# First product unit on the first quarter of x, idle products ahead of it, compression evacuation a slot later, sequences ahead of the recurrence

## The chip, the cores and the metric

The kernel runs on one core of a Trainium2 chip. The metric is the device time of one execution in microseconds. The kernel before was timed in three runs: median 2907.64 us, from 2907.31 to 2909.32. One more execution was taken by the hardware profiler; all timeline positions below are microseconds from the start of its span.

The engines are TensorE (PE in the rows; its weight loads are PEld), VectorE (DVE), ScalarE (ACT), GpSimd (POOL), and SyncE (SP), which only issues transfers. POOL issues some transfers too, on a queue of its own.

## The reference

One inference step through two layers of a hybrid decoder, all in fp32, for a prompt of 256 tokens and for 8 sample sequences of 8 new tokens each with 1024 cached tokens: 320 tokens (the N of the code), model width 2048.

```
x += layer0(norm(x)):   z = norm(x) @ w_in_e                 one projection, split into
        rx, rg              RG-LRU: conv4(rx), gates, a linear recurrence, times gelu(rg)
        q, kc,vc, ks,vs, kw,vw   attention: compressed blocks, selected blocks, window
        compress(k): per block of 64 tokens  gelu((k + pe) @ w1) @ w2      for k and for v
        out = concat(rnn, attention) @ w_out_e
x += ffn(norm(x));  x += shortconv(norm(x));  x += ffn(norm(x))       ffn: relu(x W1)^2 W2
```

For the 8 sample sequences the cached rows are in pages of 128 tokens, found through a page table. For each sequence the selected blocks, the window and the new tokens give scores, a softmax, and the weighted sum of the values.

## The kernel before, in words

**Products.** A large matrix product is `gemm` (L189). fp32 operands are held as a rounded high part and a low rest (`xh`, `xl` or `yh`, `yl` for the activations, `whi`, `wlo` for the weights), and each 128x128 block of weights takes three products of 320 columns (L204 to L206). A weight tile `wraw` of 512 KB is loaded by SP (`w_dma`, L129), then `w_conv` (L137) makes a half of it: ScalarE casts `whi` (L145), VectorE subtracts to get `wlo` (L146); for the first halves of the first four tiles GpSimd subtracts. A unit of the first layer's product is 4 chunks of the inner dimension by two blocks of 128 outputs, 24 products of TensorE. Every unit has a row of work for the other engines behind it.

**Slots and steps.** After a unit `gemm` calls `side()`, which counts up a slot and runs what `at(n, f, ...)` has registered for it, in the order of registration (L165 to L178). After every block of outputs it calls `step()`, which runs what `after(k, f)` has registered. Each engine keeps the order in which its instructions are issued; nothing reorders them later. So the order of registration is the order in which two pieces of work of one slot stand in an engine's queue.

**The start.** x comes in four quarters of 512 columns by three tensors (`xn`), with a weight tile between them. `feed(qt)` (L358) takes a quarter: `feed_a` (L341) transposes a chunk on TensorE (three transposes against the identity, the rows of L346), `feed_b` (L352) splits it into `yh` and `yl`. Quarters 0 and 1 are fed ahead of the first product, 2 and 3 behind the first and the second unit. `x_squares` sums x's squares for the norm.

**The compression.** `cmp_load_w` (L676) loads w1 and w2 for k or for v, `cmp_load` loads cached pages into `cx`, `cmp_swap` (L694) reorders them to `cy` by copies on VectorE, GpSimd and ScalarE, `cmp_mm` (L706) does 64 small products (L713) and evacuates them by ScalarE copies (L719) and VectorE adds (L720), twice each. The evacuations of q, k and v (`qr`, `kv`, L882 and L817) stand on VectorE in the same slots.

**Recurrence and sequences.** C0 = 42 is the first slot of the recurrence, which has four pairs of channel heads, eight slots apart: convolution at slots 4 and 5 behind the pair's first, gates at 5 and 6 (L584), decay at 6 (L590 to L596), scan in three parts (`rec_scan_a`, `_b`, `_c`) at 6, 7 and 8, gelu at 8 and 9, `rec_y` at 10. P4 = 65 is the first slot of the 8 sequences, three slots apart: `sa_kt` transposes cached keys to `ktl` (L1168), `sa_scores` (L1264) multiplies, `sa_softmax` (L1267) reduces and exponentiates, `sa_trans` (L1299) transposes the weights, `sa_pv` (L1312) multiplies by the values, `sa_ot` (L1335) turns the result. Where both have work in a slot (64 to 76), the recurrence, registered first, stands ahead. Slots 75 and 76 have no product unit; behind them the outputs are split and the next product, `gemm(8, 8)`, begins.

PSUM has three banks for the large products, four for the small ones (tag a) and one for others (tag o).

Of the kernel before, what the change touches and what calls it, by code (L numbers as in the profile page):

```python
# [15 lines left out]
ALU = mybir.AluOpType  # L16
# [4 lines left out]
NB = 8  # L21
# [49 lines left out]
def tile_hybrid_step(ctx: ExitStack, tc: tile.TileContext, A, O, stop=None, dbg=None):  # L71
# [57 lines left out]
    def w_dma():  # L129
        w, k, ku, c, width = units[st["dma"]]  # L130
        st["dma"] += 1
        r = wp.tile([128, UW], F32, name="wraw", bufs=NRAW)
        SP.dma_start(r[:, :ku * width].rearrange("p (k f) -> p k f", k=ku),
                     w[k * 128:(k + ku) * 128, c:c + width].rearrange("(k p) f -> p k f", p=128))
        raws.append(r)
# [29 lines left out]
    def at(n, f, *a):  # L165
        later.setdefault(n, deque()).append((f, a))
# [114 lines left out]
    for qt in range(4):  # L281
        for i in range(3):
            SP.dma_start(xn[i][:tn[i], qt * 512:(qt + 1) * 512], xsrc[i][:, qt * 512:(qt + 1) * 512])
        w_dma()
    V.memset(epst, EPS)
    S.activation(ssq[:, 0, 0:1], epst, AF.Sqrt)
    V.memset(ones, 1.0)
# [17 lines left out]


# [51 lines left out]
    def feed(qt):  # L358
        c = 4 * qt
        feed_a(c)  # L360
        feed_a(c + 1)
        if qt == 0:
            w_conv()
        feed_b(c)
        feed_a(c + 2)
        feed_b(c + 1)
        feed_a(c + 3)
        if qt == 0:
            w_conv()
        feed_b(c + 2)  # L370
        feed_b(c + 3)
# [85 lines left out]
    feed(1)  # L457
    for qt in range(3):
        at(qt, w_conv)
        at(qt, w_conv)  # L460
        if qt:
            at(qt, feed, qt + 1)
        at(qt, x_squares, qt)
    at(2, x_squares, 3)
    side(0)
# [210 lines left out]
    def cmp_load_w(i):  # L676
        nm_ = "kv"[i]
        for hf in range(2):
            SP.dma_start(w1[64 * hf:64 * hf + 64, i], A["cmp_w1_" + nm_][0][:, 32 * hf:32 * hf + 32])
        SP.dma_start(w2[64 * i:64 * i + 64, 64 * i:64 * i + 64], A["cmp_w2_" + nm_][0])  # L680
# [25 lines left out]
    def cmp_mm(bp, i, pages):  # L706
# [4 lines left out]
        for d in range(16):  # L711
            for u in range(2):
                PE.matmul(p[64 * u:64 * u + 64, :n], w1[:, i, 16 * u + d], y[:, 16 * u + d],  # L713
                          start=d == 0, stop=d == 15)
        nh = min(pages, 8)
        for k in range(pages // nh):
            h = hid[64 * i:64 * i + 64, 16 * bp + 8 * k:16 * bp + 8 * k + nh].rearrange("p n g s -> p s (n g)")
            q = p[:, 64 * k:64 * k + 8 * nh].rearrange("p (s n) -> p s n", s=2)
            S.copy(h, q[64 - 64 * i:128 - 64 * i])  # L719
            V.tensor_tensor(h, q[64 * i:64 * i + 64], h, ALU.add)  # L720
# [546 lines left out]
    def sa_softmax(b):  # L1267
# [26 lines left out]
        V.tensor_tensor(l[:, 0:2], l[:, 0:2], l[:, 2:4], ALU.add)  # L1294
        V.reciprocal(l[:, 0:2], l[:, 0:2])
        V.tensor_tensor(l[:, 0:2], l[:, 0:2], gs[:, 1:3, b], ALU.mult)
        sj["p", b] = (s, l)

    def sa_trans(b):  # L1299
# [3 lines left out]
        for i in range(4):  # L1303
            p = bank("a")
            n = min(4, 13 - 4 * i)
            for k in range(n):
                PE.transpose(p[:, 128 * k:128 * k + 128], s[:, 4 * i + k], ident)  # L1307
            (S.copy if i % 2 else V.tensor_copy)(
                t[:, 4 * i:4 * i + n].rearrange("p c k -> p (c k)"), p[:, :128 * n])
        G.tensor_scalar(t[:, 13], pcT, cm[:, C_BM + b:C_BM + b + 1], 1.0, op0=ALU.mult, op1=ALU.mult)  # L1310
# [64 lines left out]

    for pr in range(4):
# [8 lines left out]
        at(n + 8, rg_gelu_a, pr)  # L1385
        at(n + 9, rg_gelu_b, pr)
        at(n + 10, rec_y, pr)

    P4 = P3 + 20
    at(P4 - 1, sa_begin)  # L1390
    at(P4 + 1, sa_select)
    for b in range(NB + 1):
        n = P4 + 3 * b
        if b < NB:
            at(n, sa_kt, b, 0)
            at(n, sa_kt, b, 1)
        if b:
            at(n + 1, sa_trans, b - 1)
        if b < NB:
            at(n + 1, sa_kt, b, 2)  # L1400
            at(n + 2, sa_scores, b)
            at(n + 2, sa_softmax, b)
        if b:
            at(n + 2, sa_pv, b - 1)
            at(n + 4, sa_ot, b - 1)
# [286 lines left out]
```

## Time and profile before

| | |
|---|---|
| median of three runs | 2907.64 us |
| the profiled execution's own time | 2911.25 us |
| its span | 2909.6 us |
| TensorE busy | 2846.3 us, 98% of the span |
| VectorE, ScalarE, GpSimd busy | 1618.6 (56%), 1213.1 (42%), 378.2 (13%) |
| mean granted TensorE clock | 0.99 of full speed |
| mean DMA rate | 159 GB/s, 463.98 MB in all |

TensorE is busy for nearly all of the span, in the second half without a gap. In the first 600 us it is not: the products of the first layer stand there beside the attention's small work on the other engines. The granted clock is a share of full speed; of its two levels, 1.2 and 2.4 GHz, the profile's mean over a stretch is a mixture. The listed waits give the engine's instruction, the engine and instruction whose end it waited for, the sum in us, how often, and the longest.

### The profile page before, as it was taken

Reading aid. Unit: us, or ns where it says so; the run is one execution under the profiler, and the core shown is the slowest. Engines: PE = TensorE matmul, PEld = TensorE weight load, DVE = VectorE, ACT = ScalarE, POOL = GpSimd, SP = SyncE. Lnnn points to the kernel's source line nnn. Section 1 sums busy time; section 2 is a strip of 40 time slices with the busy share of each in tenths; the row PEclk is TensorE's granted clock in tenths of the full one; section 3 lists DMA queues with packets and bytes.
Section 4 is the critical chain, followed back from the end, with each engine's and each line's share of the span. In section 5 each row is a group of like instructions: output and inputs, shape, how many; then the busy total and the mean of one; then the engine's idle time right before and its main releaser. Section 6 shows DMA issues by size and latency. Waiting matters only on the chain.

```text
span 2909.6 us, 53661 instructions
## 1 busy us (share of the span) xinstructions
PE 2846.3 (98%) x20947; PEld 2785.6 (96%) x20947; DVE 1618.6 (56%) x2937; ACT 1213.1 (42%) x2336; POOL 378.2 (13%) x555
## 2 busy tenths in 40 slices
PE   8999987999999999999999999999999999999999
PEld 7998776899999999999999999999999999999999
DVE  6796677774444544544465555555444444544544
ACT  4555644354334434434443333344433433433433
POOL 2323353230010010010010111111011011001000
PEclk9999989999999999999999999999999999999999
DMA  8765258645445555555445444444444444544543
GB/s 244 213 198 156 73 147 257 210 138 162 165 154 167 165 159 161 165 166 153 153 144 156 152 147 150 147 153 148 149 152 145 153 152 149 149 152 148 149 157 119
DMA packets 275997, 463.98 MB, mean 159 GB/s; under 512 B 19050, under 2 KB 100694, under 8 KB 275215
## 3 DMA queue, kind: packets, MB, share of 16 engines
q1 hardware_dynamic: 268254, 438.47, 49.1%
q0 software_dynamic: 6864, 19.44, 2.1%
q8 instruction: 164, 2.69, 0.4%
q10 hardware_dynamic: 624, 2.64, 0.2%
q14 instruction: 91, 0.74, 0.1%
HBM read 452.95 MB, written 15.92 MB: 161 GB/s over the span
## 4 chain that ended last, share of the span: by engine, by line
PE 81%; DVE 0%; DMA 0%; ACT 0%; issue 0%; DVEq 0%; ACTq 0%
PE ps_g L204 27%; PE ps_g L206 27%; PE ps_g L205 27%; DMA wraw<-in_w_out_e_dram 0%; PE ps_a L1652 0%; DVE wlo L146 0%; PE ps_a L1264 0%; PE ps_o L1325 0%; PE ps_a L1307 0%; DVE ktl L1168 0%; PE ps_a L633 0%; PE ps_a L1624 0%; DVE rs L1473 0%; PE ps_a L436 0%; DVE y L1475 0%
## 5 line engine op out<-in xcount | busy, mean ns | idle before, releaser
L146 DVE TENSOR_TENSOR wlo<-wraw,whi 128x512 fp32r<-128x512 f32 x1488 | 1007.4, 718 | 1122.3 <-ACT whi L145 1121.5
L145 ACT CAST whi<-wraw 128x512 fp32r<-128x512 f32 x1492 | 854.1, 617 | 1377.8 <-PE ps_g L206 1334.0
L204 PE MATMUL ps_g<-yl,whi 128*128 128x320 f32 x3408 | 1066.9, 313 | 10.9 <-DVE kv L817 5.1
L205 PE MATMUL ps_g<-yh,wlo 128*128 128x320 f32 x3408 | 1056.8, 310 | 0.0
L206 PE MATMUL ps_g<-yh,whi 128*128 128x320 f32 x3408 | 1056.6, 310 | 0.0
L204 PE MATMUL ps_g<-xl,whi 128*128 128x320 f32 x2560 | 796.2, 311 | 11.3 <-DVE xl L446 7.3
L206 PE MATMUL ps_g<-xh,whi 128*128 128x320 f32 x2560 | 792.7, 310 | 0.0
L205 PE MATMUL ps_g<-xh,wlo 128*128 128x320 f32 x2560 | 792.7, 310 | 0.0
L204 PEld LDWEIGHTS ps_g<-yl,whi 128*128 128x128 f32 x3408 | 643.2, 189 | 22.3 <-issue 8.4
L205 PEld LDWEIGHTS ps_g<-yh,wlo 128*128 128x128 f32 x3408 | 643.3, 189 | 1.7 <-issue 0.2
L206 PEld LDWEIGHTS ps_g<-yh,whi 128*128 128x128 f32 x3408 | 643.2, 189 | 0.0
L204 PEld LDWEIGHTS ps_g<-xl,whi 128*128 128x128 f32 x2560 | 482.4, 188 | 13.1 <-DVE xl L446 7.7
L205 PEld LDWEIGHTS ps_g<-xh,wlo 128*128 128x128 f32 x2560 | 482.4, 188 | 0.0
L206 PEld LDWEIGHTS ps_g<-xh,whi 128*128 128x128 f32 x2560 | 482.1, 188 | 0.0
L1477 POOL TENSOR_TENSOR y<-y,rs 128x320 f32<-128x320 f32 x96 | 92.3, 994 | 1257.8 <-DVE rs L1473 1257.8
L1473 DVE TENSOR_TENSOR rs<-ps_g,r 128x320 f32<-128x320 f32 x128 | 60.6, 488 | 25.1 <-PE ps_g L206 25.0
L1506 DVE TENSOR_TENSOR fr<-fr 128x320 f32<-128x320 f32 x128 | 62.3, 487 | 11.1 <-ACT xh L1509 11.1
L431 POOL TENSOR_TENSOR nacc<-nacc,nsq 128x320 f32<-128x320 f32 x45 | 44.1, 980 | 172.0 <-ACT nsq L427 170.4
L1507 DVE TENSOR_TENSOR xl<-fr,xh 128x320 fp32r<-128x320 f32 x128 | 62.9, 492 | 4.4
L1509 ACT ACTIVATE xh<-fr 128x320 fp32r<-128x320 f32 x128 | 60.3, 471 | 4.1
L1503 ACT ACTIVATE fr<-ps_g 128x320 f32<-128x320 f32 x128 | 56.1, 438 | 5.7 <-PE ps_g L206 5.7
L1586 POOL TENSOR_TENSOR xx<-cg,r 128x256 f32<-128x256 f32 x16 | 13.1, 819 | 278.4 <-DVE xx L1584 278.4
(382 smaller groups left out, 1426.3 us busy)
## 6 DMA issues: line engine op xcount, KB each, us to landing
wraw<-in_w_ff_dram SPq DMA_DIRECT2D x512, 512.0 KB, 3.7
wraw<-in_w_in_o_dram SPq DMA_DIRECT2D x96, 512.0 KB, 3.7
wraw<-in_w_in_e_dram SPq DMA_DIRECT2D x74, 512.0 KB, 5.3
wraw<-in_w_out_e_dram SPq DMA_DIRECT2D x32, 512.0 KB, 5.5
wraw<-in_w_out_o_dram SPq DMA_DIRECT2D x32, 512.0 KB, 3.9
cx<-in_cache_cmp_k_dram SPq DMA_DIRECT2D x64, 128.0 KB, 2.1
cx<-in_cache_cmp_v_dram SPq DMA_DIRECT2D x64, 128.0 KB, 3.4
kl<-in_cache_sel_k_dram SPq DMA_DIRECT2D x64, 128.0 KB, 3.6
```

The lines of the kernel that those rows point to most:

```text
L145: S.copy(h, r)
L146: (G if u < 4 and hf == 0 else V).tensor_tensor(l, r, h.bitcast(F32), ALU.subtract)
L204: PE.matmul(ps[m][:, :N], wh, al, start=k + j == 0, stop=False)
L205: PE.matmul(ps[m][:, :N], wl, ah, start=False, stop=False)
L206: PE.matmul(ps[m][:, :N], wh, ah, start=False, stop=k + j == nk - 1)
L431: G.tensor_tensor(nacc["t"], nacc["t"], sq, ALU.add)
L1473: V.tensor_tensor(t, ps[:, :N], scale, ALU.mult)
L1477: after(1, lambda: G.tensor_tensor(y[:, c], y[:, c], t, ALU.add))
L1503: S.activation(t, ps[:, :N], AF.Relu)
L1506: V.tensor_tensor(t, t, t, ALU.mult)
L1507: V.tensor_tensor(xl[:, c], t, xh[:, c].bitcast(F32), ALU.subtract)
L1509: after(1, lambda: S.activation(xh[:, c], t, AF.Square))
```

## The change

Five parts.

First, the start: `ones` is filled first; `spin` issues products of 128x128 of `ones` by `ones` whose result nobody reads, ten at the head and one behind each chunk of quarter 0; quarters 1, 2 and 3 are fed from `after` steps 1, 3 and 5, so inside the first units; the first weight tile's transfer is two halves. Second, `cmp_load_w` uses GpSimd's queue. Third, `cmp_mm`'s evacuation is a function of its own, one copy and one add over both halves, in the next slot (the last one, of sequences 6 and 7 for v, directly). Fourth, the registration of the sequences stands ahead of that of the recurrence, and `sa_ot` a slot later in relation to `sa_trans`. Fifth, three small VectorE operations on `l` (the sum of the exps and its reciprocal, with the gates) move from the end of `sa_softmax` to the end of `sa_trans`.

```diff
@@ w_dma @@
+        nd = 2 if st["dma"] == 1 else 1
+        d = r[:, :ku * width].rearrange("p (k f) -> p k f", k=ku)
+        s_ = w[k * 128:(k + ku) * 128, c:c + width].rearrange("(k p) f -> p k f", p=128)
+        for i in range(0, ku, ku // nd):
+            SP.dma_start(d[:, i:i + ku // nd], s_[:, i:i + ku // nd])
...
@@ loads at the head @@
+    V.memset(ones, 1.0)
     V.memset(epst, EPS)
     S.activation(ssq[:, 0, 0:1], epst, AF.Sqrt)
-    V.memset(ones, 1.0)
...
+    idle = bank("o")
+
+    def spin(n):
+        for _ in range(n):
+            PE.matmul(idle[:, :128], ones, ones, start=True, stop=True)
+
+    spin(10)
+
     p0 = bank("a")
...
     def feed(qt):
         c = 4 * qt
-        feed_a(c)
-        feed_a(c + 1)
+        for i in range(4):
+            feed_a(c + i)
+            if qt == 0:
+                spin(1)
+            if i == 0 or i == 1 and qt:
+                w_conv()
+            if i:
+                feed_b(c + i - 1)
+        feed_b(c + 3)
         if qt == 0:
             w_conv()
-        feed_b(c)
-        feed_a(c + 2)
-        feed_b(c + 1)
-        feed_a(c + 3)
-        if qt == 0:
-            w_conv()
-        feed_b(c + 2)
-        feed_b(c + 3)
...
     feed(0)
-    feed(1)
+
+    for qt in range(1, 4):
+        after(2 * qt - 1, lambda qt=qt: feed(qt))
     for qt in range(3):
-        at(qt, w_conv)
-        at(qt, w_conv)
-        if qt:
-            at(qt, feed, qt + 1)
-        at(qt, x_squares, qt)
-    at(2, x_squares, 3)
-    side(0)
+        at(qt + 1, x_squares, qt)
+    at(3, x_squares, 3)
...
@@ cmp_load_w @@
-            SP.dma_start(w1[64 * hf:64 * hf + 64, i], A["cmp_w1_" + nm_][0][:, 32 * hf:32 * hf + 32])
-        SP.dma_start(w2[64 * i:64 * i + 64, 64 * i:64 * i + 64], A["cmp_w2_" + nm_][0])
+            G.dma_start(w1[64 * hf:64 * hf + 64, i], A["cmp_w1_" + nm_][0][:, 32 * hf:32 * hf + 32])
+        G.dma_start(w2[64 * i:64 * i + 64, 64 * i:64 * i + 64], A["cmp_w2_" + nm_][0])
...
@@ cmp_mm @@
+        if (bp, i) == (3, 1):
+            cmp_evac(bp, i, pages, p)
+        else:
+            at(st["slot"] + 1, cmp_evac, bp, i, pages, p)
+
+    def cmp_evac(bp, i, pages, p):
         nh = min(pages, 8)
-        for k in range(pages // nh):
-            h = hid[64 * i:64 * i + 64, 16 * bp + 8 * k:16 * bp + 8 * k + nh].rearrange("p n g s -> p s (n g)")
-            q = p[:, 64 * k:64 * k + 8 * nh].rearrange("p (s n) -> p s n", s=2)
-            S.copy(h, q[64 - 64 * i:128 - 64 * i])
-            V.tensor_tensor(h, q[64 * i:64 * i + 64], h, ALU.add)
+        h = hid[64 * i:64 * i + 64, 16 * bp:16 * bp + pages].rearrange("p (k n) g s -> p k s (n g)", n=nh)
+        q = p[:, :8 * pages].rearrange("p (k s n) -> p k s n", k=pages // nh, s=2)
+        S.copy(h, q[64 - 64 * i:128 - 64 * i])
+        V.tensor_tensor(h, q[64 * i:64 * i + 64], h, ALU.add)
...
@@ sa_softmax, sa_trans @@
-        V.tensor_tensor(l[:, 0:2], l[:, 0:2], l[:, 2:4], ALU.add)
-        V.reciprocal(l[:, 0:2], l[:, 0:2])
-        V.tensor_tensor(l[:, 0:2], l[:, 0:2], gs[:, 1:3, b], ALU.mult)
...
                 t[:, 4 * i:4 * i + n].rearrange("p c k -> p (c k)"), p[:, :128 * n])
+        V.tensor_tensor(l[:, 0:2], l[:, 0:2], l[:, 2:4], ALU.add)
+        V.reciprocal(l[:, 0:2], l[:, 0:2])
+        V.tensor_tensor(l[:, 0:2], l[:, 0:2], gs[:, 1:3, b], ALU.mult)
...
@@ the registrations of the slots (the loop over the sequences now ahead of the loop over pr) @@
+    rec_tail(3)
+    for b in range(NB + 1):
+        n = P4 + 3 * b
...
+        if b:
+            at(n + 1, sa_trans, b - 1)
+        if b > 1:
+            at(n + 1, sa_ot, b - 2)
...
+    at(n + 4, sa_ot, NB - 1)
...
-            at(n + 4, sa_ot, b - 1)
```

TensorE at the head of the program, before (`cm` holds the identity, `xn` a part of x, `pa` a parameter):

```order
L308 MATMUL ps_a<-cm,pa 128x32
L346 MATMUL ps_a<-cm,xn_113 128x128
L346 MATMUL ps_a<-cm,xn_114 128x128
L346 MATMUL ps_a<-cm,xn_115 128x64
L346 MATMUL ps_a<-cm,xn_113 128x128
```

and after:

```order
L315 MATMUL ps_o<-ones 128x128 x10
L320 MATMUL ps_a<-cm,pa 128x32
L358 MATMUL ps_a<-cm,xn_113 128x128
L358 MATMUL ps_a<-cm,xn_114 128x128
L358 MATMUL ps_a<-cm,xn_115 128x64
L315 MATMUL ps_o<-ones 128x128
L358 MATMUL ps_a<-cm,xn_113 128x128
L358 MATMUL ps_a<-cm,xn_114 128x128
```

Ten idle products stand ahead of the first transpose, and one behind the three transposes of a chunk.

The compression weights, on SP before (`w_571` is w1 and `w_572` is w2; `cx` a page of cached rows):

```order
L685 DMA cx<-in_cache_cmp_k_dram 128x256
L685 ISA
L685 DMA cx<-in_cache_cmp_k_dram 128x256
L133 DMA wraw<-in_w_in_e_dram 128x4x256
L679 DMA w_571<-in_cmp_w_k_dram 64x2048 x2
L680 DMA w_572<-in_cmp_w_k_dram 64x64
L133 DMA wraw<-in_w_in_e_dram 128x4x256
L685 ISA
L685 DMA cx<-in_cache_cmp_v_dram 128x256
```

and on GpSimd after (`w_587`, `w_588` are w1 and w2; L711 is the copy to `cy`):

```order
L940 MEMSET vn 64x256
L875 DMA out_dram<-tok 128x2x256
L879 DMA out_dram<-tok 64x256
L687 DMA w_587<-in_cmp_w_k_dram 64x2048 x2
L688 DMA w_588<-in_cmp_w_k_dram 64x64
L711 COPY cy<-cx 64x32x32 x2
```

They leave SP's queue, where eight page loads stood ahead, and come behind the stores `out_dram` on GpSimd's, ahead of a copy to `cy`.

VectorE around slots 64 and 65, before (L600 is `rec_scan_b`'s first product, L1168 the key transposes, L522 the evacuation `yr`, L1244 the first row of the block selection):

```order
L146 TENSOR_TENSOR wlo<-wraw,whi 128x512 x2
L600 SCALAR_TENSOR_TENSOR ri<-ii,ri 128x640
L1168 STREAM_TRANSPOSE ktl<-kl 128x1024 x2
L146 TENSOR_TENSOR wlo<-wraw,whi 128x512 x2
L522 TENSOR_TENSOR yr<-ps_g,rt 128x320 x2
L605 TENSOR_TENSOR xc<-xc,ri 128x640
```

and after (the same lines are L608, L1181, L530, L1257):

```order
L1248 TENSOR_TENSOR pc<-pc,mx 128x128
L603 SCALAR_TENSOR_TENSOR xc<-ii,xc 128x640
L150 TENSOR_TENSOR wlo<-wraw,whi 128x512 x2
L1181 STREAM_TRANSPOSE ktl<-kl 128x1024 x2
L608 SCALAR_TENSOR_TENSOR ri<-ii,ri 128x640
L150 TENSOR_TENSOR wlo<-wraw,whi 128x512 x2
L530 TENSOR_TENSOR yr<-ps_g,rt 128x320 x2
L1181 STREAM_TRANSPOSE ktl<-kl 128x1024
L1257 COPY pcT<-ps_a 128x128
L1259 COPY im<-ps_a 128x112
```

`ri` has moved behind two `ktl`, and a third `ktl` and the selection stand ahead of the scan.

ScalarE in the same slots, before (L584 are the gates, L590 to L596 the decay, L1232 an exp of the selection, L601 the root with its table load):

```order
L584 ACTIVATE ii<-ps_a,par 128x320
L590 ACTIVATE aa<-ri,sp_247 128x320
L591 ACTIVATE ri<-ri,sp_247 128x320
L590 ACTIVATE aa<-ri,sp_247 128x320
L591 ACTIVATE ri<-ri,sp_247 128x320
L596 ACTIVATE ii<-aa 128x640
L1232 ACTIVATE pc<-pc 128x128
L145 CAST whi<-wraw 128x512 x2
L601 ACT_TABLE_LOAD
L601 ACTIVATE ri<-ri 128x640
L145 CAST whi<-wraw 128x512 x2
```

and after (L592, L598 to L604, L1245, L609):

```order
L149 CAST whi<-wraw 128x512 x2
L1245 ACTIVATE pc<-pc 128x128
L592 ACTIVATE ri<-ps_a,par 128x320
L592 ACTIVATE ii<-ps_a,par 128x320
L598 ACTIVATE aa<-ri,sp_219 128x320
L599 ACTIVATE ri<-ri,sp_219 128x320
L598 ACTIVATE aa<-ri,sp_219 128x320
L599 ACTIVATE ri<-ri,sp_219 128x320
L604 ACTIVATE ii<-aa 128x640
L149 CAST whi<-wraw 128x512 x2
L609 ACT_TABLE_LOAD
L609 ACTIVATE ri<-ri 128x640
```

The selection's exp has moved ahead of the second pair of gates and the decay, and the casts of `whi` behind them.

## Rows read from the trace of the kernel before

**Rows 1.** Busy time of the engines (instructions), granted clock, DMA share, by stretch.
```profile
95.00:235.00 140.00, 130.83 (x1172) 125.73 (x1170) 119.13 (x150) 69.97 (x104) 34.26 (x25) 0.98 0.65 192
400.00:494.00 94.00, 71.24 (x987) 61.89 (x984) 75.37 (x183) 45.23 (x92) 38.83 (x67) 0.87 0.78 236
600.00:2909.00 2309.00, 2304.69 (x15724) 2302.37 (x15722) 1172.55 (x1967) 909.17 (x1696) 180.08 (x243) 1.00 0.49 153
```

**Rows 2.** What TensorE waited for in 0 to 600.
```profile
PE ps_a L1307 <- ACT ot_s L1342: 7.1, 1, 7.1
PE ps_a L1264 <- DVE ktl L1168: 5.7, 1, 5.7
PE ps_g L204 <- DVE kv L817: 5.1, 2, 4.2
PE ps_a L713 <- DMA w<-in_cmp_w_k_dram: 4.1, 1, 4.1
PE ps_g L204 <- DVE y L1432: 4.1, 3, 2.0
PE ps_g L204 <- DVE qr L882: 4.0, 2, 2.9
```

**Rows 3.** Timeline of TensorE, 0 to 32: start, duration, instruction, idle before.
```profile
4.43 0.48 PE L346 MATMUL ps_a<-cm,xn 128*128 128x128 f32 x1 [1.03 <-DMA xn<-in_x_prompt_dram]
...
10.79 3.11 PE L346 MATMUL ps_a<-cm,xn 64*128 64x64 f32 x10 [0.32 <-DMA xn<-in_x_sample_dram]
13.83 0.63 PE L204 MATMUL ps_g<-yl,whi 128*128 128x320 f32 x1
...
19.50 0.31 PE L204 MATMUL ps_g<-yl,whi 128*128 128x320 f32 x1
19.65 0.31 PE L205 MATMUL ps_g<-yh,wlo 128*128 128x320 f32 x1
...
19.94 2.30 PE L346 MATMUL ps_a<-cm,xn 128*128 128x128 f32 x12
...
25.79 2.29 PE L346 MATMUL ps_a<-cm,xn 128*128 128x128 f32 x12
```

**Rows 4.** Timeline of TensorE, the first and the third call of `cmp_mm`.
```profile
71.76 6.45 PE L713 MATMUL ps_a<-cy,w 128*64 128x128 f32 x64 [4.07 <-DMA w<-in_cmp_w_k_dram]
...
101.31 3.71 PE L713 MATMUL ps_a<-cy,w 128*64 128x128 f32 x64
```

**Rows 5.** Timeline of SP's issues, the load of w1.
```profile
60.19 1.16 SPq L679 DMA_DIRECT2D w<-in_cmp_w_k_dram  x2
```

**Rows 6.** Timeline of VectorE, the copies to `cy` ahead of the first `cmp_mm`.
```profile
62.41 3.97 DVE L703 COPY cy<-cx 64x1024 f32<-64x1024 f32 x2 [1.97 <-issue]
```

**Rows 7.** Timeline of GpSimd, the copies to `cy`.
```profile
51.79 2.04 POOL L703 COPY cy<-cx 64x1024 f32<-64x1024 f32 x1 [0.36 <-issue]
62.42 3.00 POOL L703 COPY cy<-cx 64x1024 f32<-64x1024 f32 x1 [8.59 <-DMA cx<-in_cache_cmp_k_dram]
```

**Rows 8.** What VectorE waited for in 95 to 235.
```profile
DVE yr L720 <- ACT yr L719: 6.0, 9, 3.0
```

**Rows 9.** Timeline of VectorE, the key transposes of sequence 0.
```profile
406.71 2.37 DVE L1168 STREAM_TRANSPOSE ktl<-kl 128x1024 f32<-128x1024 f32 x2
```

**Rows 10.** Timeline of ScalarE, 399 to 411: decay, casts, table load.
```profile
398.98 0.64 ACT L590 ACTIVATE aa<-ri,sp 128x320 f32<-128x320 f32 x1
...
401.45 0.72 ACT L596 ACTIVATE ii<-aa 128x640 f32<-128x640 f32 x1
...
403.11 0.60 ACT L145 CAST whi<-wraw 128x512 fp32r<-128x512 f32 x1
...
406.88 1.28 ACT L601 ACT_TABLE_LOAD   x1 [1.54 <-DVE ri L600]
...
408.81 1.12 ACT L145 CAST whi<-wraw 128x512 fp32r<-128x512 f32 x2
```

**Rows 11.** What VectorE waited for in 400 to 494.
```profile
DVE l L1294 <- ACT sp L1292: 6.2, 4, 1.6
DVE sp L1288 <- POOL yr L625: 3.4, 1, 3.4
```

More of the change, by code (lines that the diff above doesn't have):

```diff
@@ L132, in w_dma @@
         r = wp.tile([128, UW], F32, name="wraw", bufs=NRAW)
-        SP.dma_start(r[:, :ku * width].rearrange("p (k f) -> p k f", k=ku),
-                     w[k * 128:(k + ku) * 128, c:c + width].rearrange("(k p) f -> p k f", p=128))
+        nd = 2 if st["dma"] == 1 else 1
[3 more added lines that the diff above has]
+            SP.dma_start(d[:, i:i + ku // nd], s_[:, i:i + ku // nd])
         raws.append(r)
@@ L1374, in tile_hybrid_step, with rec_tail @@
     at(P3 + 18, p3_close)
+    P4 = P3 + 20
+    at(P4 - 1, sa_begin)
+    def rec_tail(pr):
+        n = C0 + 8 * pr
+        at(n + 8, rg_gelu_a, pr)
+        at(n + 9, rg_gelu_b, pr)
+        at(n + 10, rec_y, pr)
+    rec_tail(3)
+    for b in range(NB + 1):
+        n = P4 + 3 * b
+        if b < NB:
+            at(n, sa_kt, b, 0)
+            at(n, sa_kt, b, 1)
+        if b:
+            at(n + 1, sa_trans, b - 1)
+        if b > 1:
+            at(n + 1, sa_ot, b - 2)
+        if b < NB:
+            at(n + 1, sa_kt, b, 2)
+            at(n + 2, sa_scores, b)
+            at(n + 2, sa_softmax, b)
+        if b:
+            at(n + 2, sa_pv, b - 1)
+    at(n + 4, sa_ot, NB - 1)
+    at(P4 + 1, sa_select)
     for pr in range(4):
@@ L1384, in tile_hybrid_step @@
             at(n + 6 + i, f, pr)
[L1385 to L1404, printed above, removed]
-            at(n + 4, sa_ot, b - 1)
+        if pr < 3:
+            rec_tail(pr)
     def rx_or_rg(g, m, ps):
```

## The prediction, written before the changed kernel had run

> **What bounds the kernel now.** I read the windows of the span first, then the list of what TensorE waits for, then the timelines of the three places where waits sit. From 600 us on TensorE is busy 2304.69 of 2309 us at full clock, and nothing that the change moves runs there [rows 1]: 79% of the span cannot move, and every microsecond to be won or lost lies ahead of 600. There the waits are few and named [rows 2]: one on the compression weights (4.1), one on the 13th transpose of a sequence's weights (7.1), one on the key transposes `ktl` (5.7), four on the evacuation of k, v and q (5.1 + 4.0), three on `y` (4.1). In 400-494 VectorE is busy 75.37 of 94 us and TensorE 71.24 [rows 1], so in that stretch VectorE's queue, and not TensorE, sets the pace: a TensorE wait removed there comes back at the next place where TensorE needs VectorE, unless VectorE's own idle time goes with it. In 95-235 it is 119.13 of 140, much the same.
>
> The sum is made against the profiled execution: 2911.25 us, of which 2909.6 is span. The median of the three runs is 2907.64, so 3.6 lower; I take the change in time over to it as it is.
>
> **Start (0-28 us).** Before, 24 transposes precede the first product at 13.83; the products come 0.27 us apart (21 of them between 13.83 and 19.50) and 0.15 apart after that, which is half and full clock (1.2 and 2.4 GHz) [rows 3]. (The granted clock column says 1.00 for the whole start; the spacing contradicts it and I go by the spacing.) Transposes cost 3.11 / 10 = 0.31 at half clock and 2.30 / 12 = 0.19 at full. Four quarters and two units, 48 transposes and 48 products, are through at 28.08. After the change there are ten idle products at the head and one behind each chunk of the first quarter, and the feeds of the other quarters lie between the products. The idle products have no row: 128 columns in fp32, like a transpose, so 0.19 to 0.31 each by the nearest rows, up to 0.48 by the full-size transpose at half clock [rows 3]. Ten take 3 to 5 us from about 1.2 us on, and the first transpose stood at 4.43, so between nothing and 0.8 us of it is in the way. Bounds: if the idle products raise the clock, all is at the full price from 5.5 us on, 48 x 0.19 + 48 x 0.15 + 4 x 0.19 = 17.1, through at 22.6, a gain of 5.5. If the clock never rises among mixed transposes and products, it is 48 x 0.31 + 48 x 0.27 + 4 x 0.31 = 29.1, through at 34.6, a loss of 6.5. If it rises after as many products as before (4 x 0.31 + 24 x 0.31 + 21 x 0.27, then 24 x 0.19 + 27 x 0.15), it is 5.5 + 14.4 + 8.6 = 28.5, a loss of 0.4. VectorE and ScalarE must also deliver the split x and weights 4 us sooner. I take +2, near the middle between -0.4 and +5.5, since 12 transposes at 19.94 did not lower a clock that was up.
>
> The Trainium skill speaks against this (TensorE: Matmul & The Clock Gate, Part 4: PE-mode transpose): work in transpose mode does not count as TensorE being busy for the clock. The trace agrees ahead of 13.83, where transposes leave the first products at half clock, and is silent on transposes with one product in four [rows 3]. By that rule the start would tend to the loss of 6.5, and the sum to the third rival's.
>
> **Compression weights on GpSimd's queue (54-78 us).** Before, SP issues them at 60.19, behind eight page loads, and TensorE waits 4.07 us at 71.76 for their landing; the 64 products then take 6.45, at half clock, where the same 64 take 3.71 at 101.31 [rows 4, 5]. After, POOL issues them ahead of a copy `cy` that ended at 53.83, before POOL idled 8.59 us [rows 7]; that idle time covers three issues, each about as long as SP's (1.16 / 2), and the weights ask for the memory some six us sooner than from SP. With them landed, what comes last is VectorE's `cy` copies, 62.41 to 66.38 [rows 6], and TensorE's own earlier work to 67.69, where its wait began. So the 4.07 goes, and with no idle stretch the clock should hold: 6.45 - 3.71 = 2.74. Sum +6.8. Bounds: +4.1 if the products stay cold, 0 if the transfers, 1 MB either way, only delay the weight tiles of the products, +9 if the next wait on `yr` goes too. I take 6.8.
>
> **Compression evacuation a slot later (95-235 us).** Two copies and two adds become one and one, queued behind the k/v or q evacuation. VectorE stands 6.0 us in 9 waits for these copies [rows 8], ahead of the evacuations for which TensorE then waits 5.1 + 4.0 [rows 2]. If all of the latter went, +9; if VectorE, 85% busy there, only refills the time with work that was late anyway, 0; -2 if the PSUM bank, held one slot longer, comes late. Two thirds of the 6.0: +4.
>
> **Sequences ahead of the recurrence (400-494 us).** The registration order decides who goes first in a slot. Step by step on VectorE and ScalarE:
> - `ri`, the recurrence's input product, now stands behind two `ktl` (2.37 us) instead of ahead of them [rows 9]. ScalarE's table load waits for `ri` (1.28), and the root and the next two casts follow it to 409.9 [rows 10]; before, all this ran beneath the two `ktl`. After, VectorE's next `wlo` waits for about 1.28 + 0.65 + 0.6 = 2.5 us, where it hardly waited: -2.3. The evacuation `yr` behind it is later by that, and TensorE with it.
> - ScalarE's second gate pair, decays and `ii` (four of 0.64 and one of 0.72, to 402.17) now stand behind `pc`'s exp, and so 3.3 us more are ahead of the next cast, at 403.11 before [rows 10]. VectorE's other work covers part: -2.
> - `ktl` moves ahead of the block selection and the scan, so TensorE's 5.7 us wait [rows 2] goes; but the softmax that follows needs VectorE, which has as much ahead of it as before. 0.
> - The first shift recurs at pair 3: -2.3; and there the convolution's casts come behind a softmax's exps on ScalarE, with TensorE's gates waiting for them: -2.5, an estimate by the size of the first shift.
> - The `l` operations go from the softmax to behind the transposes: VectorE's four waits of 1.55 for the exps (6.2 in all) shrink [rows 11], but the next `wlo` needs a cast that stands behind the same exps: +2 of 6.2.
> - The `ot_s` copy comes behind the transposes, so the 7.1 us wait goes; VectorE idles 3.4 of that [rows 11], which is what can be won: +3.4.
>
> Sum -3.7, taken as -4. Bounds: +12.8 if both waits (5.7 + 7.1) go and nothing comes in their place; -8 if no cover holds.
>
> **Behind 494** the same order gives back part of the waits on `y` (4.1, [rows 2]) and adds a wait of `sa_ot`: +1, between -2 and +4.
>
> Sum: 2 + 6.8 + 4 - 4 + 1 = 9.8. The profiled execution would be 2901.4, the median 2897.8, about 2898. The likeliest case by itself is 2893 to 2902.
>
> **Rivals.** *The sequences' order pays in full.* Both large waits go and VectorE's idle time, 94 - 75.37 = 18.6 us, takes up the rest: 12.8 in place of -4, so 2881. For it: the two waits are the longest of the program. Against: in 400-494 VectorE has 80% of the time in work, and in the middle of the 5.7 us wait it did not rest.
>
> *The recurrence starves (slower).* At slot 64 to 74 its chain is behind each sequence's work, and as TensorE waits more often, the clock falls: it was 0.87 there already [rows 1]. A unit of 24 products costs 24 x (0.27 - 0.15) = 2.9 more at half clock; with six units so and the -8 of the bound, -25. It decides from -20 on, where the other gains (13.8) are outweighed by more than 0.2%; the time would be 2907.64 + 25 - 13.8 = 2919. Against: before, only some of these units were cold.
>
> *The start stays cold.* The loss of 6.5 in place of +2: sum 1.3, 2906.3, within what can be told from no change. For it, transposes that do not raise the clock; against, ten products ahead of them.
>
> *The change does nothing of what it says*, each gain given back by VectorE's queue: 2907.6.
>
> **How the numbers follow.** A measurement of this kernel tells 0.2%, 5.8 us, from no change. Forecast 0.46, order pays in full 0.18, cold start 0.22, starved recurrence 0.12, nothing 0.02. Faster is the first two, 0.64; the same is the cold start and nothing, 0.24; slower 0.12. The range takes the upper half of the second case and reaches past the unchanged median into the lower bounds of the fourth: 2885 to 2911.
>
> **What would show it.** Start: the first product's time and spacing, near 10 us and 0.15 apart if the clock rose; 48 transposes and 48 products through before 26. Compression: the first of the 64 products near 66 to 68 with no wait on a DMA, and 3.7 us long. Evacuation: less TensorE wait for k, v and q than 9.1 in 95-235, and no waits of VectorE for the copy. Sequences: no wait for `ktl`, a longer VectorE wait for `whi` behind the table load, and gemm(8, 8) starting 3 to 5 us later than before relative to the end of the previous stretch. The forecast is wrong if TensorE's idle time in 400-494 falls by more than 6 us, or if the products before 28 us stay 0.27 apart.

## The result and the profile after

The changed kernel takes 2922.31 us (median of five runs, 2919.57 to 2924.39) against 2907.31 for the kernel before in the same runs: a ratio of 1.0051, 95% interval 1.0038 to 1.0064, so 15 us slower where 10 us faster was forecast. The profiled execution took 2923.16 us, its span is 2921.5, its mean granted clock 0.988.

The same three stretches as in [rows 1], of the changed kernel (PE, PEld, DVE, ACT, POOL busy, granted clock, DMA share, GB/s):

```profile
95.00:235.00 140.00, 131.10 (x1173) 125.58 (x1172) 117.14 (x146) 70.50 (x100) 32.97 (x25) 0.98 0.63 190
400.00:494.00 94.00, 65.35 (x954) 55.96 (x954) 70.35 (x162) 40.43 (x81) 35.53 (x59) 0.85 0.69 199
600.00:2909.00 2309.00, 2309.00 (x15756) 2307.18 (x15756) 1174.09 (x1968) 913.40 (x1704) 183.41 (x248) 1.00 0.49 153
```

In 400-494 TensorE is busy 65.35 us where it was 71.24, and VectorE 70.35 where it was 75.37. These 94 us do not hold the same work, because the changed kernel falls behind in them. The stretch between two evacuations does, from `rxb` (385.59 before, 387.76 after) to the first `y` (500.15 and 513.56); before, then after:

```profile
385.59:500.15 114.56, 91.80 (x1185) 79.56 (x1190) 90.43 (x210) 54.43 (x110) 52.04 (x87) 0.90 0.73 219
```

```profile
387.76:513.56 125.80, 90.20 (x1198) 77.88 (x1201) 93.80 (x210) 53.96 (x110) 52.20 (x87) 0.88 0.69 202
```

It is 11.2 us longer. TensorE is busy for about as long, so what came on top is waiting of TensorE (22.8 us before, 35.6 after) and not products at half clock. VectorE waits more as well, 32.0 us where it was 24.1.

TensorE's waits in 0 to 620, against [rows 2] (which leaves out a wait for `xl`, 7.3 before):

```profile
PE ps_a L1277 <- DVE ktl L1181: 13.0, 3, 8.0
PE ps_a L1354 <- DVE pT L1318: 8.7, 1, 8.7
PE ps_g L208 <- DVE xl L457: 7.1, 2, 5.4
PE ps_g L208 <- DVE yr L530: 6.0, 3, 5.4
PE ps_a L721 <- DVE yr L711: 5.3, 1, 5.3
PE ps_g L208 <- DVE qr L895: 4.6, 3, 3.4
...
PE ps_g L208 <- DVE kv L830: 4.3, 2, 3.5
```

The wait for `w` (4.1) is gone and the one for `yr` of the compression (L711) is 5.3, where it was 2.5; the wait for `ot_s` (7.1) is one for `pT` (8.7); the wait for `ktl` (5.7) is 13.0; and 5.4 for the evacuation `yr` (L530) are new. The waits for q and k, v are 8.9 where they were 9.1. Where the two kernels stand at the same evacuation shows when the time goes. Minus is ahead of the kernel before, in us, start times of VectorE's instruction in the two profiles:

| evacuation, at (before) | after minus before |
|---|---|
| first `kv`, 36.18 | +2.6 |
| `kv`, 82.14 | -4.4 |
| `kv`, 112.43 | -1.1 |
| `kv`, 226.63 | -1.0 |
| `rxb`, 385.59 | +2.2 |
| `yr`, 410.67 | +6.2 |
| `yr`, 468.48 | +10.4 |
| first `y`, 500.15 | +13.4 |
| `y`, 596.87, and from there to the end | +12.0 |

The profile of before that stands in [rows 1] was a long one of its kind (2911.25 against a median of 2907.31), which is why these 12 are 3 less than the medians' 15. Positions up to `rxb` vary by several us from execution to execution (see the second profile of before, below), so only the growth behind it is clear.

**The start**, on TensorE's timeline, against [rows 3]:

```profile
1.20 4.41 PE L315 MATMUL ps_o<-ones 128*128 128x128 f32 x20 [1.20 <-DVE epst L290]
5.54 0.24 PE L320 MATMUL ps_a<-cm,pa 32*128 32x32 f32 x1
...
9.60 0.41 PE L208 MATMUL ps_g<-yl,whi 128*128 128x320 f32 x1
9.85 0.31 PE L209 MATMUL ps_g<-yh,wlo 128*128 128x320 f32 x1
...
15.97 2.29 PE L358 MATMUL ps_a<-cm,xn 128*128 128x128 f32 x12
...
39.32 0.63 PE L208 MATMUL ps_g<-yl,whi 128*128 128x320 f32 x1 [1.34 <-DVE kv L828]
39.75 0.47 PE L209 MATMUL ps_g<-yh,wlo 128*128 128x320 f32 x1
```

The idle products (recorded as two each) take 4.41 us and after them the clock is full: the first products, at 9.60, are 0.15 apart, and 12 transposes between products take 2.29. So 12 transposes between products did not bring the clock down here. By 33.24 the first 96 products are through, 35.32 before: the +2 forecast. Then a spell at half clock (products 0.27 apart, from 36.02 on) and a wait for the first `kv` evacuation give back 4.

**The compression.** The first group of 64 small products starts at 70.54 and takes 3.71 us, the price of full clock in [rows 4]; the second waits:

```profile
70.54 3.71 PE L721 MATMUL ps_a<-cy,w 128*64 128x128 f32 x64 [0.96 <-DVE cy L711]
86.78 3.61 PE L721 MATMUL ps_a<-yr,w 128*64 128x24 f32 x64 [5.29 <-DVE yr L711]
```

On VectorE's timeline is what it waits for: the position rows, two loads of 64 KB that SP still issues.

```profile
85.65 2.02 DVE L711 COPY yr<-tok 64x384 f32<-64x384 f32 x4 [4.97 <-DMA tok<-in_cmp_pe_k_dram]
```

**The sequences**, on VectorE's timeline in slots 64 to 66, against [rows 9]:

```profile
408.77 1.30 DVE L150 TENSOR_TENSOR wlo<-wraw,whi 128x512 fp32r<-128x512 f32 x2 [2.78 <-ACT whi L149]
409.98 2.36 DVE L1181 STREAM_TRANSPOSE ktl<-kl 128x1024 f32<-128x1024 f32 x2
412.27 0.78 DVE L608 SCALAR_TENSOR_TENSOR ri<-ii,ri 128x640 f32<-128x640 f32 x1
415.70 1.29 DVE L150 TENSOR_TENSOR wlo<-wraw,whi 128x512 fp32r<-128x512 f32 x2 [2.65 <-ACT whi L149]
416.91 0.88 DVE L530 TENSOR_TENSOR yr<-ps_g,rt 128x320 f32<-128x320 f32 x2
```

and on ScalarE's, against [rows 10]:

```profile
403.99 0.31 ACT L1245 ACTIVATE pc<-pc 128x128 f32<-128x128 f32 x1 [5.44 <-DVE pc L1244]
...
408.13 1.12 ACT L149 CAST whi<-wraw 128x512 fp32r<-128x512 f32 x2
413.13 1.28 ACT L609 ACT_TABLE_LOAD   x1 [3.87 <-DVE ri L608]
...
415.06 1.12 ACT L149 CAST whi<-wraw 128x512 fp32r<-128x512 f32 x2
```

ScalarE stands 5.44 us before `pc`'s exp with the gates behind it, and 3.87 before the table load with the casts behind it; VectorE waits 2.78 and 2.65 for those casts. In 400-494 VectorE's two largest waits are:

```profile
DVE wlo L150 <- ACT whi L149: 14.4, 6, 2.8
DVE sp L1301 <- PE ps_a L1277: 4.1, 2, 3.1
```

The four waits of `l` for the exps (6.2 in [rows 11]) are gone, and the waits for `whi`, 1.6 us before, are 14.4.

### The profile page after: what moved, and what is told of

Same layout as the page of the kernel before. It is cut to its first block, busy times and chain, and to the rows that moved or that the text cites. A ratio compares the mean times of both kernels' runs of the same rounds, so it can differ in the third digit from the quotient of the medians.

```text
span 2921.5 us, 53720 instructions
## 1 busy us (share of the span) xinstructions
PE 2847.5 (97%) x20975; PEld 2788.2 (95%) x20975; DVE 1615.8 (55%) x2929; ACT 1212.5 (42%) x2328; POOL 379.2 (13%) x561
## 4 chain that ended last, share of the span: by engine, by line
PE 87%; DVE 5%; DMA 3%; issue 2%; SPq 2%; ACT 1%; POOL 0%; DVEq 0%; ACTq 0%; POOLq 0%
PE ps_g L208 28%; PE ps_g L209 28%; PE ps_g L210 28%; DVE wlo L150 1%; DVE cy L711 1%; PE ps_a L721 1%; SPq L693 1%; PE ps_a L1277 1%; SPq L668 1%; DMA wraw<-in_w_in_e_dram 0%; DMA kl<-in_cache_win_k_dram 0%; DMA cx<-in_cache_cmp_v_dram 0%; PE ps_o L1338 0%; DVE hrs L847 0%; DMA c<-in_c_dram 0%
```

## The experiments

Theory A: the order of the sequences is the loss, by VectorE's waits for casts that stand behind what they used to run beneath; the other parts come to little, because each removed wait comes back at the next late thing. The rivals are named in each expectation. Medians, of 5 to 12 executions each, are against the 2906.6 to 2907.2 of the kernel before in the same runs.

### Each part by itself

**The order** (registration of the sequences ahead, and `sa_ot` behind the transposes):

```diff
+    rec_tail(3)
+    for b in range(NB + 1):
...
     for pr in range(4):
```

> The kernel before with only the new registration order of the sequences, the recurrence and sa_ot. Theory A (the order is the loss: VectorE waits for whi behind pc's exp and behind the table load, 2.8 and 2.65 us twice over in the changed kernel's trace): 9 to 13 us slower than before, median 2916 to 2920, TensorE's wait for yr near slot 65 about 5 us. Theory B (the order costs the 4 that was forecast, the rest of the loss is the start and spells of half clock): 2 to 6 us slower, 2909 to 2913. Theory C (the order gains, as its two removed waits say): 5 us faster or more.

Measured 2921.08, ratio 1.0054 (1.0041 to 1.0067): 14 us slower, a little more than theory A's 9 to 13; the wait for `yr` is 5.4 as it says. From `rxb` to the first `y`:

```profile
379.76:507.15 127.39, 92.67 (x1198) 78.27 (x1202) 92.17 (x211) 53.84 (x110) 54.69 (x91) 0.88 0.68 201
```

That is 12.8 us more than before, 12.0 of it idle time of TensorE (34.7 against 22.8). In eight profiles without an edit in this stretch, the two of before among them, it takes 113.8 to 116.1.

**All but the order:**

```diff
-    rec_tail(3)
-    for b in range(NB + 1):
...
+    for b in range(NB + 1):
```

> The changed kernel with the old registration order (start, weights on GpSimd, later evacuation and the l operations stay). Theory A: the loss goes, 2904 to 2912, within 0.2% of before; in its trace the delay at 396 us is 0 to 3 us and does not grow to 494. Theory B: 2914 to 2918, still clearly slower.

Measured 2913.18, 1.0018 (1.0009 to 1.0027): 6 us slower than before, between the two expectations' ranges. The order is most of the loss and not all of it; the other parts together cost as well. None of these 6 lies between `rxb` and the first `y`, which takes 114.07 here.

**The start:**

```diff
+    spin(10)
...
+        after(2 * qt - 1, lambda qt=qt: feed(qt))
```

> The kernel before with only the new start. Theory A (the start wins 2 us by 33 us, and the later squares of x push the first kv evacuation on VectorE 2.6 us back, which TensorE pays at half clock): 1 to 3 us slower than before, 2908 to 2910. Theory B (the start's gain holds, what was lost by 50 us came from other parts): 2 us faster, 2905.

Measured 2909.06, 1.0009 (1.0000 to 1.0017): the gain of the first 33 us does not last, and the time is in theory A's range; by the interval the loss is not clear of nothing.

**The weights:**

```diff
-            SP.dma_start(w1[64 * hf:64 * hf + 64, i], ...)
+            G.dma_start(w1[64 * hf:64 * hf + 64, i], ...)
```

> The kernel before with only the compression weights on GpSimd's queue. Theory A (the 4.1 us wait and the cold products go, and most stays won until 100 us): 3 to 7 us faster, 2900 to 2904. Theory B (VectorE's next cy and yr copies give it back, as the changed kernel's 5.29 us wait for yr says): within 2 us of before.

Measured 2910.45, 1.0012 (1.0004 to 1.0021): neither; it is slower by 3.6. VectorE waits 4.0 us for the position rows in its trace, and TensorE 4.7 for `yr`:

```profile
DVE yr L703 <- DMA tok<-in_cmp_pe_k_dram: 4.0, 1, 4.0
```

**The evacuation:**

```diff
+            at(st["slot"] + 1, cmp_evac, bp, i, pages, p)
```

> The kernel before with only the compression evacuation a slot later and merged. Theory A (VectorE's 6.0 us of waits for the copies go and two thirds reach TensorE): 3 to 5 us faster. Theory B (VectorE only refills the time with work that is late anyway, and other waits on qr and kv stay at 8 us or more in 95 to 235): within 2 us of before.

Measured 2904.43, 0.9993 (0.9984 to 1.0001): 2.7 us faster, not clear of nothing. In its trace VectorE's waits for the copy fall little, those for `whi` grow from 5.9 to 9.4, and TensorE's for q, k and v are 8.9 where they were 9.1, as theory B says:

```profile
DVE wlo L146 <- ACT whi L145: 9.4, 5, 3.6
DVE yr L725 <- ACT yr L724: 4.9, 1, 4.9
```

**The `l` operations:**

```diff
-        V.tensor_tensor(l[:, 0:2], l[:, 0:2], l[:, 2:4], ALU.add)     # in sa_softmax
+        V.tensor_tensor(l[:, 0:2], l[:, 0:2], l[:, 2:4], ALU.add)     # in sa_trans
```

> The kernel before with only the l operations moved behind the transposes. Forecast: 2 us faster, because VectorE's four waits of 1.55 us for the exps shrink. Rival: 0 or slower, because the next wlo waits for a cast that stands behind the same exps, and the three operations now lie ahead of the third ktl.

Measured 2907.52, 1.0000 (0.9991 to 1.0009): nothing, as the rival said. In its trace the waits for the exps (6.2 in [rows 11]) are gone from 400 to 494, and those for `whi` are 5.7 there, where they were 1.6.

The five by themselves are +14.2, +2.2, +3.6, -2.7 and +0.6: 18 against the 15 of all together.

### What in the order costs

**Recurrence first again, but for the scan's last part** (in the order-only kernel):

```diff
+    for pr in range(4):
+        at(n + 4, rec_conv, 2 * pr)
...
+        at(n + 7, rec_scan_b, pr)
+
     P4 = P3 + 20
```

> The order-only kernel with one thing put back: convolution, gates, decay and the scan's first two parts registered ahead of the sequences again (the scan's third part and the gelu stay behind; sa_ot as in the change). Theory A (the loss is VectorE's waits for whi behind pc's exp and behind the table load, about 2.7 us four times): 6 to 11 of the 14 us come back, 2910 to 2915. Theory B (the loss is the key transposes and selection ahead of the scan's third part): at most 4 come back, 2917 to 2921.

Measured 2913.28, 1.0019 (1.0010 to 1.0028): 8 of the 14 us come back. In its trace VectorE's waits for `whi` in 396 to 500 are 3.8 us, 12.8 in the order-only kernel's.

**The scan's second part alone, and the gates and decay alone:**

```diff
+        at(n + 7, rec_scan_b, pr)
```

> The order-only kernel (2921.1) with only the scan's second part (ri and the root with its table load) registered ahead of the sequences again. Theory A (each of the two shifts carries about half of the 8 us): 2916 to 2918. Rival (the table load behind ri carries it all): 2912 to 2914.

Measured 2918.26, 1.0043 (1.0029 to 1.0056): 3 back.

```diff
+        at(n + 4, rec_conv, 2 * pr)
...
+        at(n + 6, rec_decay, pr)
+        at(n + 6, rec_scan_a, pr)
```

> The order-only kernel with only convolution, gates, decay and the scan's first part registered ahead again; the scan's second and third part stay behind. Theory A: 2916 to 2918. Rival (the cast behind pc's exp and the gates carries it all): 2912 to 2914; if neither part alone gives anything, the two wait for each other.

Measured 2917.16, 1.0037 (1.0024 to 1.0051): 4 back. With five executions each, the 3 and the 4 are rough. The traces agree with them, from `rxb` to the first `y`, in us:

| | the stretch | TensorE idle in it | its wait for `yr` near 410 |
|---|---|---|---|
| before | 114.56 | 22.8 | none listed |
| order only | 127.39 | 34.7 | 5.4 |
| scan's second part first | 125.33 | 28.7 | 3.2 |
| gates and decay first | 125.87 | 30.7 | 2.8 |
| both first | 119.25 | 23.6 | none listed |

So each shift carries its share, and both together bring TensorE's idle time back to that of before. What is left of the longer stretch with both first, 4.7, is busy time, 95.66 against 91.80, at a clock of 0.86 against 0.90.

**`sa_ot` alone behind the transposes, and put back:**

```diff
-            at(n + 4, sa_ot, b - 1)
+        if b > 1:
+            at(n + 1, sa_ot, b - 2)
```

> The kernel before with only sa_ot behind the transposes of the next sequence. Theory A (TensorE's 7.1 us wait was for VectorE's queue at slot 72, not for the ot_s copy, and comes back as a wait for the copy pT): within 3 us of before, with a wait of 6 us or more for pT on sa_ot near 475. Theory B (the wait goes): 4 to 7 us faster.

Measured 2910.02, 1.0007 (0.9998 to 1.0015): no gain, and not clear of nothing as a loss. The wait has a new name only:

```profile
474.64 0.48 PE L1341 MATMUL ps_a<-cm,or 128*64 128x64 f32 x4 [7.46 <-DVE pT L1308]
```

> The recurrence-first variant of the order (2913.3) with sa_ot back where it was. Theory A (the later sa_ot costs about 3 us, as it did by itself): 2909 to 2911. Rival (the rest of the loss is the third scan part behind the key transposes and the selection): 2912 to 2914.

Measured 2910.89, 1.0015 (1.0005 to 1.0024): 2.4 less than the variant above; the intervals overlap, so it agrees with some 3 us for `sa_ot` without proving it. What of the edit is left in this variant is the scan's third part and the gelu behind the sequences, and the selection behind the key transposes; neither was tried by itself. Its TensorE idles 24.0 us from `rxb` to the first `y`, near the 22.8 of before, so the 4 that are left do not show as waiting of TensorE, and their cause is open.

**Load taken from VectorE** (on the evacuation-only kernel):

```diff
-        (G if u < 4 and hf == 0 else V).tensor_tensor(l, r, h.bitcast(F32), ALU.subtract)
+        (G if (u < 4 or 66 <= u < 78) and hf == 0 else V).tensor_tensor(l, r, h.bitcast(F32), ALU.subtract)
```

> The evacuation-only kernel, and for weight tiles 66 to 77 (the slots of the sequences) GpSimd instead of VectorE subtracts the first half's low part, 12 of 0.68 us taken from VectorE. Theory A (VectorE's queue is what sets the pace in 400 to 494): 3 to 8 us faster than the evacuation alone (2904.4), so 2896 to 2902. Theory B (it is the chain of waits between engines, and VectorE's load does not matter): within 2 us of it, or slower by the longer GpSimd subtraction.

Measured 2912.05, 1.0020 (1.0010 to 1.0029): slower by nearly 8 than the evacuation alone. It does not test VectorE's load, because VectorE was hardly relieved. Its subtractions in 400 to 494 in the evacuation-only kernel (count, then busy and mean ns of one):

```profile
L146 DVE TENSOR_TENSOR wlo<-wraw,whi 128x512 fp32r<-128x512 f32 x22 | 14.9, 715 | 0.9 <-ACT whi L145 0.9
```

and in this one, GpSimd's first in a fence of its own:

```profile
L146 POOL TENSOR_TENSOR wlo<-wraw,whi 128x512 fp32r<-128x512 f32 x11 | 15.2, 1384 | 8.2 <-issue 8.0
```

```profile
L146 DVE TENSOR_TENSOR wlo<-wraw,whi 128x512 fp32r<-128x512 f32 x10 | 12.5, 1254 | 1.1 <-ACT whi L145 1.1
```

The mean of 1254 ns is not that of each: seven of the ten take 0.64 to 0.69 us, and the three that fall beside GpSimd's work 1.05, 1.88 and 4.92. The longest lasted until four instructions of GpSimd, one behind the other, had ended (the first and the last of them are shown):

```profile
427.89 4.92 DVE L146 TENSOR_TENSOR wlo<-wraw,whi 128x512 fp32r<-128x512 f32 x1
```

```profile
427.87 1.56 POOL L625 TENSOR_TENSOR yr<-ii,yr 128x640 f32<-128x640 f32 x1
...
430.99 1.26 POOL L146 TENSOR_TENSOR wlo<-wraw,whi 128x512 fp32r<-128x512 f32 x1
```

How these add up to 8 us is not shown.

### The start, the weights, and a second profile of before

**The squares later:**

```diff
-    at(3, x_squares, 3)
+    at(4, x_squares, 3)
+    at(4, norm_sums)
```

> The start-only kernel with the squares of the last quarter of x, and the sum of the squares, a slot later, behind the first kv evacuation. Theory A (the start's gain was lost by the squares ahead of that evacuation): 2 us faster than start-only (2909.1), so 2906 to 2908, and no wait of TensorE for kv near 37. Theory B: 2908.5 to 2910.

Measured 2910.67, 1.0018 (1.0008 to 1.0027). That is above both ranges. My reason falls: with the squares behind the evacuation TensorE still waits 1.86 us for it, and the spell of half clock is there as well.

**The kernel before again:**

> The kernel before unchanged, for a second profile. If the spells of half clock lie at other places from execution to execution of one kernel: the same order and the same waits, but one or more of the spells near 371, 402 and 528 us gone or moved, and delays between the two profiles of 1 to 3 us that arise in stretches without any difference in order. If they belong to the order of the work, the two profiles agree within 0.3 us at every evacuation.

Measured 2906.61, 0.9999 (0.9990 to 1.0007), and its profile is 3.1 us ahead of the first one by 600 us, with the same instructions: 1.5 lie at 112 already, and 2.5 near 371, where the first profile has a spell of half clock (granted clock 0.75 in 366 to 376) and this one has none (1.00). So two single profiles differ by such amounts without any cause in the order.

Seven variants above leave everything ahead of the sequences as it was (order only, its three partial returns, `sa_ot` late, `sa_ot` put back, the `l` operations). With the two profiles of before that makes nine of the same instructions in the same order up to 380 us. They differ more:

| | the nine | with the new start (four, two of them with the other parts) |
|---|---|---|
| first 96 products through | 34.54 to 36.45 | 31.66 to 33.24 |
| granted clock in 34 to 44 | 1.00 in three, 0.83 in six | 0.66 |
| `kv`, 47.71 in the first profile | 47.71 to 49.90 | 48.25 to 49.61 |
| `kv`, 112.43 | 106.24 to 113.53 | 107.97 to 112.02 |
| `rxb`, 385.59 | 378.44 to 386.58 | 378.56 to 387.76 |

So the first profile is a late one, and being ahead or behind it by a few us at 112 or at 385 says nothing of an edit. The gain of the start at 33 us is clear of this, its loss by 48 as well, and so is a longer spell of half clock in between; that a spell falls there at all is not the edit's doing.

In 255 to 267, where the order of the instructions is the same, before was at full clock and the changed kernel was not:

```profile
255.00:267.00 12.00, 11.87 (x90) 11.14 (x89) 9.23 (x38) 3.30 (x6) 10.59 (x23) 1.00 1.02 280
```

```profile
255.00:267.00 12.00, 12.00 (x71) 11.55 (x71) 8.22 (x36) 2.42 (x5) 9.59 (x21) 0.72 1.05 269
```

The second profile of before has 1.00 there too, and all but the order 0.72, so this spell may come with the other parts by their timing; that is not shown.

**The position rows on GpSimd's queue too:**

```diff
-            SP.dma_start(x[0:64, 2], A["cmp_pe_" + ...
+            G.dma_start(x[0:64, 2], A["cmp_pe_" + ...
```

> Evacuation, compression weights and also the two small loads of the position rows on GpSimd's queue. Theory A (the weights' gain was lost because VectorE waited 4.05 us for the position rows, which SP issues at 80.7): TensorE's wait for yr near 87 falls from 4.7 to 2.5 us or less, 3 to 6 us faster than the evacuation with weights would be, so 2900 to 2904. Theory B (the loss of the weights has another cause): 2906 to 2911.

Measured 2903.62, 0.9990 (0.9981 to 1.0000), in theory A's range, but no more than 0.8 below the evacuation alone. The DMA wait is gone, and TensorE's wait does not fall as theory A says: it still waits 4.13 us at 83.34, now for VectorE's own copies `cy` and `yr` (8 us on end).

**And the small product a slot later:**

```diff
-        at(E["vc"] + (7 if i else 5), cmp_mm, 4, i, 3)
+        at(E["vc"] + (7 if i else 6), cmp_mm, 4, i, 3)
```

> The kernel with the evacuation, the weights and the position rows changed, and the small product of the new tokens for k a slot later, so that 24 large products lie between VectorE's yr copies and their use. Theory A (with the transfers early, VectorE's copies are what comes late there, TensorE waits 4.1 us for them at 83): that wait falls under 1 us and the time to 2898 to 2901, 5 to 9 us faster than before. Theory B (the wait only moves): 2902 to 2905.

Measured 2900.05 (2897.34 to 2903.36), 0.9980 (0.9971 to 0.9989): 6.6 us faster than before and 22 than the change, as theory A says; 4.4 of the 6.6 lie beyond the evacuation alone. TensorE in 54 to 95, before and here:

```profile
54.00:95.00 41.00, 34.41 (x281) 32.80 (x281) 27.09 (x33) 19.68 (x27) 11.83 (x9) 0.83 0.90 239
```

```profile
54.00:95.00 41.00, 40.81 (x420) 39.66 (x419) 32.86 (x35) 21.54 (x29) 19.45 (x19) 1.00 0.94 267
```

No wait over 0.2 us is left there and the clock is full. At `rxb` this kernel stands at 373.61, ahead of all nine profiles above. The later small product was not tried without the rest.

## Why the prediction was wrong

Between 10 faster and 15 slower lie 25 us. Two steps make some 10 each, the sum for the sequences and the gain of the weights; the start misses by 4 and the evacuation by 1.

**The first step that failed is the sum for the sequences: -4 forecast, -14 measured.** Its losing terms were nearly right. Of the waits that it worked out, 2.3 and 2 at the first shift and 2.3 at pair 3 stand in the changed trace as VectorE's waits for `whi` of 2.65, 2.78 and 2.65, at the places named. The 2.5 for the convolution behind a softmax's exps does not (VectorE waits 0.52 there); in its place the casts behind pair 3's gates and decay cost 2.29. Undoing these shifts gives 8 us back. The two at pair 3:

```profile
468.66 1.29 DVE L150 TENSOR_TENSOR wlo<-wraw,whi 128x512 fp32r<-128x512 f32 x2 [2.29 <-ACT whi L149]
...
477.61 1.29 DVE L150 TENSOR_TENSOR wlo<-wraw,whi 128x512 fp32r<-128x512 f32 x2 [2.65 <-ACT whi L149]
```

Its winning terms were wrong, both by the reasoning that it used against the rival but not on itself:
- "The `ot_s` copy comes behind the transposes, so the 7.1 us wait goes": +3.4 forecast, -3 measured (at best 0). VectorE has `pT` behind the scan and two `ktl` in either order, and TensorE waits for it instead, 7.46 in the variant with this edit alone. Nor do the 3.4 us of VectorE's idle time lie in the wait that was to go. In the profile of before TensorE's wait ends at 476.51; VectorE works through it, copies `pT` in it, and stands idle only behind it, until TensorE's next scores (to 480.40) and GpSimd's `yr` (to 480.59) are done:

```profile
476.51 0.45 PE L1307 MATMUL ps_a<-cm,sp 128*128 128x128 f32 x1 [7.12 <-ACT ot_s L1342]
```

```profile
474.43 1.25 DVE L1308 COPY pT<-ps_a 128x512 f32<-128x512 f32 x2
...
480.59 0.62 DVE L1288 CUSTOM_DVE_ANT_1 sp<-ps_a,badd,mnew 128x384 f32<-128x384 f32 x1 [3.37 <-POOL yr L625]
```

- "+2 of 6.2" for the `l` operations: nothing; the waits for the exps became waits for the casts behind them.
- The key transposes ahead of the selection and the scan, put at 0: what they cost, if anything of the last 4 us, is not shown.

**The second step that failed is the gain of the weights: +6.8 forecast, -3.6 measured.** The first wait and the cold products went as said: the 64 products start at 70.54 and take 3.71. The step stopped at the first next-late thing, VectorE's `cy`, and did not ask for the second: the position rows' loads on SP, then VectorE's copies, then the slot of the small product. With those three moved, and the evacuation as well, the kernel is 6.6 us faster than before, 4.4 faster than with the evacuation alone. That the part alone is slower than nothing, and not just even, is not explained: its profile has 110.31 at the `kv` of 112.43 and 383.23 at `rxb`, inside the range of the nine.

**The evacuation: +4 forecast, +2.7 measured**, with an interval that reaches nothing. TensorE's waits for q, k and v stayed at 8.9, so what there is of a gain did not come the way I said.

**The start: +2 forecast, and 2.1 at 33 us**, by the mechanism named: idle products raised the clock, and the first product came at 9.6. It is lost by 50 us, to a longer spell of half clock behind 34 and the wait for the first `kv` evacuation; the squares are not why. What makes the clock fall there, in six of the nine profiles without the edit as well, stays open.

**Behind 494** the forecast +1 is not shown. The delay falls from 13.4 at the first `y` evacuation to 12.0 at 597, but from one to the other order-only needs 96.89 us, and the two profiles of before 96.72 and 97.48.

The third rival, a start that stays cold, is refuted by the spacing of the products. The starved recurrence, with a chance of 0.12, came nearest, at 2919. It was right in the place and in the waits, but that its time is so near is luck: some 17 of its 25 us were units at half clock, and TensorE's busy time between `rxb` and the first `y` did not grow in the changed kernel; and it kept 13.8 us of other gains that did not come. What I did not see is that the case I forecast has the same losing terms as this rival, and that the gains set against them were ones I had granted myself.

## What to carry to other kernels

Where two engines take turns, ask of a wait of one that ends on the other's queue whether a new order removes it or only moves it, as here with `ot_s`, the `l` operations and the weights; count as won only what leaves the longer queue. Before moving a chain that ends in a table load or an exp behind other work, list what used to run beneath it: casts queued behind it are now uncovered. For each wait that goes, follow the same consumer to the second and third late thing; here the edit paid once all of them had moved. And compare two profiles over a stretch between the same two instructions: positions alone carry everything that varied before.

## What the runs showed of the hardware

A subtraction of 128x512 on VectorE takes 0.64 to 0.69 us by itself; three beside GpSimd's work took 1.05, 1.88 and 4.92, the last until a run of four GpSimd instructions had ended. In 400 to 494 the sharing gave 2.4 us to VectorE for 15.2 of GpSimd's. Ten idle products of 128x128, 4.41 us, left TensorE at full clock ahead of work that had begun at half. And nine profiles of the same instructions differ by 7.3 us at 112 us: the granted clock up to there is 0.98 in the earliest and 0.94 in the latest, and their waits differ as well. So a change of a few us needs medians, and one profile of each kernel mainly tells which waits there are.
